# Sums of two parts of a matrix, moved from GpSimd adds to a copying and an accumulating transfer, and two masks built earlier

## The chip, the cores and the metric

The kernel runs on one core of one Trainium2 chip. The metric is the device time of one execution in microseconds (us). TensorE (PE) does the matrix products, VectorE (DVE), ScalarE (ACT) and GpSimd (POOL) the elementwise work. SyncE (SP), ACT and POOL also issue transfers (DMA), and all transfers run on the same 16 DMA engines of the core.

## What is computed

Two layers on a sequence of 512 tokens with 1024 features, and a last normalisation, all in fp32. The second layer, gated linear attention (GLA), stands around the change:

```python
h = h + ssd_mixer(rmsnorm(h, ssd_norm), ...)      # layer 1
h = h + gla_mixer(rmsnorm(h, gla_norm), ...)      # layer 2
return rmsnorm(h, final_norm)

def gla_mixer(u, w_in, w_gate, b_gate, onorm, w_out):
    q, k, v, z, gl = split(u @ w_in)               # gl: 2 x 16 columns, the low-rank gate
    lg = log_sigmoid(gl @ w_gate + b_gate) / 16
    o = gla_scan(q, k, v, lg[0]) + rev(gla_scan(rev(q), rev(k), rev(v), rev(lg[1])))
    return (rmsnorm(o, onorm) * silu(z)) @ w_out
```

## The kernel before

Every product of fp32 matrices is made of three matmuls (`mm3`, L150): each operand is held as a high part (a rounded copy, made by ACT) and a low part (the difference, made by DVE); high times high, high times low and low times high are added in PSUM. For weights, `Weights` loads 512 KB at a time through SP into `wraw` (3 buffers), ACT makes `whi` (L89) and DVE makes `wlo` (L90), 3 buffers each. A buffer of `whi` or `wlo` is free again when PE has read it. For the layer's input u the parts are `uh` and `ul`, 128 x 8 x 512 each, kept for the whole layer.

Layer 1 (SSD) uses the pool `sp`; at its end `proj_out_rows` (L826) adds the layer's output to `h` for each of four blocks of 128 tokens, and `norm2` normalises the block, transposes it on PE and splits it into `uh` and `ul` (L157). Then the pool `gp` takes over the same memory for layer 2.

Layer 2 makes v and z of each head by a product of 2 x 2 blocks with 7 instead of 8 block products (`vz_part`, L881). That needs sums of blocks of u, and these need u itself again, `uf` = `uh` + `ul`, in two tiles (`ufgyh` for features 0 to 511 and `ufgyl` for 512 to 1023), each of 128 x 4 x 512. `uf` is written in four pieces of 128 x 4 x 256 (512 KB), by GpSimd. The order of pieces is: first half of the tokens of `ufgyh`, then of `ufgyl`; second half of `ufgyh`, then of `ufgyl`. From them `sums_of_u` (L848) makes

```python
x = a22 - a21          # L853: second token half of ufgyl minus second token half of ufgyh
y = -x - a11           # L850: a11 is the first token half of ufgyh
# split of y into s2h, s2l and of x into q5h, q5l
x = a11 - a21          # L857, split into s3h, s3l
y = -y - a12           # L850, split into s4h, s4l; a12: first token half of ufgyl
```

In the text "tx" and "ty" are the DVE instructions that write x and y. The program order of the first head is: block products a11 (result `m1`, copied out of PSUM by ACT at L907) and a12 (L893 adds `m1`: `gc`, then split into `vh`, `vl`); `gate_low` (L950), the product for gl with a weight of 768 columns (`pch` with 96 rows, L72 loads its weight); q and k (two more `pch`); the gates (`ptg`, L961, needs `gl` from ACT and DVE, L952 and L953, and `wgs`, the split gate weights of L938 and L939, loaded into `wgr` by SP at L934 after GpSimd has cleared it at L932); then the blocks s2, q5, s3, a22, s4. Products that stay in PSUM take tiles of the tag `mm`, which has 4 buffers (L142): the product of `gate_low` takes the buffer that held the first result of a11, and so starts after the copy of `m1`.

The instructions of an engine run in one fixed order, which a list scheduler has worked out from the program with its own cost estimates. `mk3` (which is the tile `one`, changed in place) and `mle` (`lef` in between) are two 128 x 128 masks; `mle` is first used at L1062.

Of the kernel before, what the change touches and what calls it, by code (L numbers as in the profile page):

```python
# [10 lines left out]
F32 = mybir.dt.float32  # L11
F32R = mybir.dt.float32r
U8 = mybir.dt.uint8
AF = mybir.ActivationFunctionType
ALU = mybir.AluOpType

P = 128
# [30 lines left out]
class Weights:  # L48
# [64 lines left out]
    def next(self):  # L113
        n = len(self.specs) if self.limit is None else self.limit
        while self.n_spl < n and self.n_spl <= self.pos + LOOK_SPL:
            while self.n_raw <= self.n_spl:
                self._load(self.n_raw)
                self.n_raw += 1
            with self.tc.high_priority(offset=SPLIT_AHEAD):
                self._split(self.n_spl)  # L120
            self.n_spl += 1
        self.load_ahead()
        i = self.pos
        for f in self.beside.pop(i, ()):
            f()
        self.pos += 1
        return self.spl.pop(i)


def build(tc, I, out):  # L130
    nc = tc.nc
    ctx = ExitStack()
    with ctx:
        cp = ctx.enter_context(tc.tile_pool(name="cp", bufs=1))
# [36 lines left out]
        def small_loads():  # L171
# [10 lines left out]
        idn = cp.tile([P, P], F32, name="idn")  # L182
        make_identity(nc, idn)
        one = cp.tile([P, P], F32, name="one")
# [3 lines left out]
        ge = cp.tile([P, P], F32, name="ge")  # L188
        nc.gpsimd.affine_select(
            out=ge, in_=one, pattern=[[1, P]], compare_op=ALU.is_ge, fill=0.0, base=0, channel_multiplier=-1  # L190
        )
        mlt = cp.tile([P, P], U8, name="mlt")
        nc.vector.tensor_scalar(out=mlt, in0=ge, scalar1=0.5, scalar2=None, op0=ALU.is_lt)
        rmf = cp.tile([P, L], F32, name="rmf")
        nc.vector.memset(rmf, 1.0)
        nc.vector.memset(rmf.rearrange("p (c l) -> p c l", l=P)[:, :, 0:1], 0.0)
# [55 lines left out]
        class Blocks:  # L252
# [8 lines left out]
            def step(self, n):  # L261
                w = self.w
                dst, src, add = (
                    (w["w1"], self.b11, False),
                    (w["w3"], self.b12, False),
                    (w["w1"], self.b12, True),
                    (w["w3"], self.b22, True),
                    (w["w2"], w["w1"], False),
                    (w["w2"], self.b22, True),
                    (w["w4"], w["w2"], False),  # L270
                    (w["w4"], self.b21, True),
                )[n]
                if add:
                    dma = nc.gpsimd.dma_start(dst, src, accum_op=ALU.add)
                else:
                    dma = nc.gpsimd.dma_start(dst, src)
                tc.add_manual_dep(
                    dma.ins, W.mark.ins.name,
                    mybir.DependencyInfo(mybir.DependencyClass.Sync, mybir.DependencyReason.DATA),
                    reason="pace",  # L280
                )
# [32 lines left out]
        uh = cp.tile([P, KD, L], F32R, name="uh")  # L314
        ul = cp.tile([P, KD, L], F32R, name="ul")
# [48 lines left out]
        def proj_tok(step=lambda: None):  # L364
            pts = [mmb(f"ptk{t}") for t in range(NT)]
            for kk in range(4):
                if kk:
                    step()
                wh, wl = W.next()
                for t in range(NT):  # L370
                    sl = slice(t * P, (t + 1) * P)
                    for j in range(2):
                        k = 2 * kk + j
                        mm3(pts[t], (uh[:, k, sl], ul[:, k, sl]), (wh[j], wl[j]), k == 0, k == KD - 1)
            return pts
# [64 lines left out]
        with tc.tile_pool(name="sp", bufs=1, reuse_waits="tile") as sp:  # L440
# [108 lines left out]
            def proj_group(g, step):  # L549
                b = conv_silu(proj_ch(), 16 + g, "bch")  # L550
                step()
                c = conv_silu(proj_ch(), 24 + g, "cch")
                step()
                x0 = conv_silu(proj_ch(), 2 * g, "xch")
                step()
                x1 = conv_silu(proj_ch(), 2 * g + 1, "xch")
                return b, c, x0, x1

            def z_gate(pts, pool, n):
                zs = []  # L560
                for t in range(NT):
                    if t % 2 == 0:
                        zs.append(pool.tile([P, 2, 512], F32, tag="zs", name=f"zs{t}", bufs=n))
                    z = zs[-1][:, t % 2]
                    nc.scalar.activation(z, pts[t], AF.Tanh, scale=0.5)
                    nc.vector.scalar_tensor_tensor(
                        out=z, in0=z, scalar=1.0, in1=pts[t], op0=ALU.add, op1=ALU.mult
                    )
                return zs
# [224 lines left out]
            for g in range(G + 1):  # L794
                it = iter(scan_group(g - 1, grp.pop(g - 1), zs[(g - 1) // 2])) if g else iter(())
                left = [SCAN_STEPS, 4 * ((g % 2 == 0 and g < G) + (g < G) + (g in (3, 5, 8)))]

                def step():
                    n = -(-left[0] // max(left[1], 1))
                    left[0] -= n  # L800
                    left[1] -= 1
                    for _ in range(n):
                        next(it, None)

                if g < G:
                    if g % 2 == 0:
                        zs[g // 2] = z_gate(proj_tok(step), sp, 3)
                        step()
                    if g == 0:
                        dt_part()  # L810
                        for i in range(3):
                            load_bc(i)
                    grp[g] = proj_group(g, step)
                    step()
                if g in (3, 5, 8):
                    proj_out(yts1(g // 2 - 1 if g < 8 else 2), step)
                for _ in it:
                    pass
# [11 lines left out]
        with tc.tile_pool(name="gp", bufs=1, reuse_waits="tile") as gp:  # L830
            uf = [gp.tile([P, 4, L], F32, tag=tg, name=f"uf{tg}") for tg in ("gyh", "gyl")]
            for th in range(2):
                for hf in range(2):
                    sl = (slice(None), slice(hf * 4, hf * 4 + 4), slice(th * 256, th * 256 + 256))
                    nc.gpsimd.tensor_tensor(
                        out=uf[hf][:, :, sl[2]], in0=uh[sl].bitcast(F32), in1=ul[sl].bitcast(F32), op=ALU.add
                    )


            f1, f2 = slice(0, 256), slice(256, 512)  # L840
# [95 lines left out]
            for d in range(2):  # L936
# [1 line left out]
                nc.scalar.copy(w, wgr[d])  # L938
                nc.vector.tensor_tensor(out=w[32:64], in0=wgr[d][32:64], in1=w[32:64].bitcast(F32), op=ALU.subtract)  # L939
                wgs.append(w)  # L940
            mk3 = one
            nc.vector.tensor_tensor(out=mk3, in0=one, in1=idn, op=ALU.add)
            lef = gp.tile([P, P], F32, tag="xx0", name="lef")
            nc.vector.tensor_tensor(out=lef, in0=mk3, in1=ge, op=ALU.subtract)
            mle = gp.tile([P, P], U8, name="mle")
            nc.vector.tensor_scalar(out=mle, in0=lef, scalar1=0.5, scalar2=None, op0=ALU.is_gt)

            gl = gp.tile([96, L], F32R, name="gl")

# [246 lines left out]
```

## Time and profile before

| | us |
|---|---|
| median of 3 runs | 869.54 (869.53 to 871.34) |
| the profiled execution | 871.69 |
| its span in the trace | 870.0 |
| PE busy in it | 840.9 |
| DVE busy | 676.3 |
| ACT busy | 505.1 |
| POOL busy | 88.5 |

The profiled execution is 2.15 us above the median. The times of the rows below count from the start of its span. A busy time of an engine is a sum over the whole program; what a change in one stretch does is read from who waits for whom in that stretch.

### The profile page before, as it was taken

What the parts mean: (1) busy time and instruction counts of PE and PEld (TensorE: products, weight loads), DVE (VectorE), ACT (ScalarE), POOL (GpSimd) and SP (SyncE); (2) the same over time, 40 slices, a digit from 0 to 9 for tenths busy, and PEclk for the clock granted to TensorE, in tenths of its full rate; (3) what the DMA queues carried; (4) which work ended last, traced back from release to release, by engine and by line L of the source; (5) the groups of instructions that cost most, each with busy time, mean ns of one, the idle gap of its engine ahead of it and who ended that gap; (6) DMA issues with size and microseconds to landing.
All of it is one profiled execution on the core that took longest, in us unless ns stands there. A gap on an engine that the chain in (4) does not pass through costs nothing.

```text
span 870.0 us, 11270 instructions
## 1 busy us (share of the span) xinstructions
PE 840.9 (97%) x3982; PEld 688.3 (79%) x3982; DVE 676.3 (78%) x1046; ACT 505.1 (58%) x1074; POOL 88.5 (10%) x156
## 2 busy tenths in 40 slices
PE   8998999999999999999998999999999999999996
PEld 5786888887888888888877767878888888887875
DVE  6488988999768986589896789859953996399744
ACT  4337587756766566567574547557524762385333
POOL 2002011101101011110101320010001000100012
PEclk9999999999999999999999999999999999999998
DMA  6447848967878687696530236406530662155202
GB/s 211 129 112 298 209 140 234 252 151 231 208 222 218 171 235 199 174 262 170 146 121 25 67 105 178 138 24 185 156 95 27 179 182 74 48 162 177 98 1 97
DMA packets 90198, 132.92 MB, mean 153 GB/s; under 512 B 7969, under 2 KB 49149, under 8 KB 87966
## 3 DMA queue, kind: packets, MB, share of 16 engines
q1 hardware_dynamic: 76844, 83.83, 31.9%
q0 software_dynamic: 11424, 34.74, 17.5%
q10 hardware_dynamic: 1874, 13.64, 4.1%
q8 instruction: 31, 0.51, 0.2%
q14 instruction: 25, 0.20, 0.1%
HBM read 129.96 MB, written 35.78 MB: 191 GB/s over the span
## 4 chain that ended last, share of the span: by engine, by line
PE 63%; DVE 14%; ACT 10%; issue 5%; DMA 3%; POOL 3%; SPq 0%; POOLq 0%; ACTq 0%; DVEq 0%
PE pch L152 5%; PE pch L151 5%; PE pch L153 5%; PE po L153 4%; PE po L151 4%; PE po L152 4%; DVE wlo L90 4%; PE pb L151 3%; PE pb L153 3%; PE pb L152 3%; PE pyi L713 3%; ACT whi L89 3%; PE ptk L151 3%; PE ptk L153 2%; PE ptk L152 2%
## 5 line engine op out<-in xcount | busy, mean ns | idle before, releaser
L90 DVE TENSOR_TENSOR wlo<-wraw,whi 128x1024 fp32r<-128x1024 f32 (+1 forms) x114 | 140.3, 1232 | 56.3 <-ACT whi L89 56.0
L89 ACT CAST whi<-wraw 128x1024 fp32r<-128x1024 f32 (+1 forms) x114 | 118.7, 1041 | 95.7 <-PE pch L152 30.2
L153 PE MATMUL pch<-uh,wlo 128*128 128x512 f32 (+2 forms) x336 | 133.4, 397 | 0.8 <-DVE wlo L90 0.7
L151 PE MATMUL pch<-uh,whi 128*128 128x512 f32 (+2 forms) x336 | 133.7, 398 | 0.0
L152 PE MATMUL pch<-ul,whi 128*128 128x512 f32 (+2 forms) x336 | 132.8, 395 | 0.0
L153 PEld LDWEIGHTS pch<-uh,wlo 128*128 128x128 f32 (+2 forms) x336 | 62.5, 186 | 15.3 <-DVE wlo L90 1.7
L152 PEld LDWEIGHTS pch<-ul,whi 128*128 128x128 f32 (+2 forms) x336 | 62.5, 186 | 13.9 <-issue 0.3
L151 PEld LDWEIGHTS pch<-uh,whi 128*128 128x128 f32 (+2 forms) x336 | 62.5, 186 | 13.5
L541 DVE SCALAR_TENSOR_TENSOR cv<-pch,colA,cv 128x511 f32<-128x511 f32 (+1 forms) x96 | 70.5, 742 | 0.2
L94 ACT ACTIVATE whi<-wraw,colB 128x512 fp32r<-128x512 f32 x58 | 39.1, 717 | 43.8 <-PE pch L152 25.3
L151 PE MATMUL ptk<-whi,uh 128*128 128x512 f32 x128 | 51.4, 406 | 0.0
L153 PE MATMUL ptk<-whi,ul 128*128 128x512 f32 x128 | 50.5, 396 | 0.0
L152 PE MATMUL ptk<-wlo,uh 128*128 128x512 f32 x128 | 50.5, 396 | 0.0
L95 DVE SCALAR_TENSOR_TENSOR wlo<-wraw,colB,whi 128x512 fp32r<-128x512 f32 x58 | 41.7, 748 | 9.9 <-ACT whi L94 8.5
L318 POOL TENSOR_SCALAR rs<-ss 128x2 f32<-128x2 f32 (+1 forms) x32 | 8.6, 268 | 382.0 <-ACT gy L1097 270.2
L680 ACT ACTIVATE bct<-bct,eb 128x128 f32<-128x128 f32 x128 | 42.1, 395 | 6.3 <-DVE bct L677 6.3
L672 ACT ACTIVATE bct<-bct,eb 128x128 f32<-128x128 f32 x128 | 41.2, 395 | 3.4 <-DMA bct<-cumd 3.4
L151 PE MATMUL pb<-whi,uh 128*128 128x512 f32 x96 | 38.7, 403 | 3.2 <-DVE u L893 2.0
L152 PE MATMUL pb<-wlo,uh 128*128 128x512 f32 x96 | 38.3, 399 | 0.0
L153 PE MATMUL pb<-whi,ul 128*128 128x512 f32 x96 | 38.1, 397 | 0.0
L151 PE MATMUL po<-whi,yh 128*128 128x512 f32 x96 | 37.9, 396 | 0.1
L152 PE MATMUL po<-wlo,gyh 128*128 128x512 f32 x96 | 37.9, 395 | 0.0
(308 smaller groups left out, 2022.9 us busy)
## 6 DMA issues: line engine op xcount, KB each, us to landing
wraw<-in_ssd_w_in_dram SPq DMA_DIRECT2D x48, 512.0 KB, 5.7
wsumw<-in_gla_w_in_dram POOLq DMA_DIRECT2D x24, 1024.0 KB, 9.6
wraw<-in_gla_w_in_dram SPq DMA_DIRECT2D x32, 512.0 KB, 3.8
wraw<-wsumw SPq DMA_DIRECT2D x32, 512.0 KB, 3.5
bct<-cumd ACTq DMA_DIRECT2D x13, 1024.0 KB, 6.6
wraw<-in_ssd_w_out_dram SPq DMA_DIRECT2D x16, 512.0 KB, 5.3
wraw<-in_gla_w_out_dram SPq DMA_DIRECT2D x16, 512.0 KB, 4.0
bct<-cumd SPq DMA_DIRECT2D x3, 1024.0 KB, 14.0
```

The source lines that it names most:

```text
L89: self.mark = nc.scalar.copy(vh, raw)
L90: nc.vector.tensor_tensor(out=vl, in0=raw, in1=vh.bitcast(F32), op=ALU.subtract)
L94: self.mark = nc.scalar.mul(hs[j], raw[:, j], g)
L95: nc.vector.scalar_tensor_tensor(out=ls[j], in0=raw[:, j], scalar=g, in1=hs[j].bitcast(F32), op0=ALU.mult, op1=ALU.subtract)
L151: nc.tensor.matmul(pt, lhsT=a[0], rhs=b[0], start=first, stop=False)
L152: nc.tensor.matmul(pt, lhsT=a[0], rhs=b[1], start=False, stop=False)
L153: W.mm = nc.tensor.matmul(pt, lhsT=a[1], rhs=b[0], start=False, stop=last)
L318: nc.gpsimd.tensor_scalar(out=dst, in0=ss, scalar1=mul, scalar2=add, op0=ALU.mult, op1=ALU.add)
L541: nc.vector.scalar_tensor_tensor(out=cv[:, o0:o1], in0=pt[:, o0 + s : o1 + s], scalar=cwt(j, a), in1=cv[:, o0:o1], op0=ALU.mult, op1=ALU.add,)
L672: nc.scalar.activation(bct[:, r], bct[:, r], AF.Identity, bias=TM["eb"][:, cc, i : i + 1])
L680: nc.scalar.activation(et[:, r], et[:, r], AF.Exp, bias=TM["eb"][:, cc, i : i + 1])
L713: nc.tensor.matmul(py[:, q * 256 + r * 64 : q * 256 + (r + 1) * 64], lhsT=et[:, r], rhs=xt[:, cc, r * 64 : (r + 1) * 64], start=True, stop ...
```

## The change

Each of the four adds of GpSimd is replaced by two transfers of 512 KB inside the on-chip memory: one issued by ACT that copies a piece of `uh` into `uf`, and one issued by GpSimd that adds the piece of `ul` to it on its way. The three instructions for the masks move into the loop of layer 1 (at g == 4), with `lef` in a buffer of the tag `jk` and `mle` in the pool that lives for the whole kernel.

```diff
+        mk3, mle = one, cp.tile([P, P], U8, name="mle")
...
+                if g == 4:
+                    nc.vector.tensor_tensor(out=mk3, in0=one, in1=idn, op=ALU.add)
+                    lef = sp.tile([P, P], F32, tag="jk", name="lef", bufs=2)
+                    nc.vector.tensor_tensor(out=lef, in0=mk3, in1=ge, op=ALU.subtract)
+                    nc.vector.tensor_scalar(out=mle, in0=lef, scalar1=0.5, scalar2=None, op0=ALU.is_gt)
...
             for th in range(2):
                 for hf in range(2):
                     sl = (slice(None), slice(hf * 4, hf * 4 + 4), slice(th * 256, th * 256 + 256))
-                    nc.gpsimd.tensor_tensor(
-                        out=uf[hf][:, :, sl[2]], in0=uh[sl].bitcast(F32), in1=ul[sl].bitcast(F32), op=ALU.add
-                    )
+                    nc.scalar.dma_start(uf[hf][:, :, sl[2]], uh[sl].bitcast(F32))
+                    nc.gpsimd.dma_start(uf[hf][:, :, sl[2]], ul[sl].bitcast(F32), accum_op=ALU.add)
...
-            mk3 = one
-            nc.vector.tensor_tensor(out=mk3, in0=one, in1=idn, op=ALU.add)
-            lef = gp.tile([P, P], F32, tag="xx0", name="lef")
-            nc.vector.tensor_tensor(out=lef, in0=mk3, in1=ge, op=ALU.subtract)
-            mle = gp.tile([P, P], U8, name="mle")
-            nc.vector.tensor_scalar(out=mle, in0=lef, scalar1=0.5, scalar2=None, op0=ALU.is_gt)
```

The order of PE's instructions stays as it was. On ACT, DVE, POOL and SP it changes around the passage from layer 1 to layer 2.

ACT before, from the split of the last normalised block on (`whi` of 768 is the weight of `gate_low`; the two `whi` of 1024 after it are those of q and k):

```order
L156 CAST uh<-ptn 128x4x128 [waits PE_49] x2
L89 CAST whi_4542<-wraw_4538 128x768 [waits DMAHW4_49,DMAHW3_49,DMAHW5_49,PE_49,Activation_49]
L907 COPY m_4532<-pb_4486 128x512
L89 CAST whi_4560<-wraw_4558 128x1024 [waits DMAHW6_49,PE_49,Activation_49]
L907 COPY m_4533<-pb_4487 128x512
L156 CAST q5h<-tx 128x1024 [waits DVE_49]
L156 CAST s2h<-ty 128x1024 [waits DVE_49]
L89 CAST whi_4600<-wraw_4598 128x1024 [waits DMAHW7_49,PE_49,Activation_49]
```

ACT in the changed kernel at the same place (DMAHW with a number is the completion counter of one of eight groups of transfers that SP and ACT issue):

```order
L156 CAST uh<-ptn 128x4x128 [waits PE_49] x2
L841 DMA ufgyh<-uh 128x4x256 [waits DVE_49]
L89 CAST whi_4546<-wraw_4542 128x768 [waits DMAHW4_49,DMAHW3_49,DMAHW5_49,PE_49,Activation_49]
L841 DMA ufgyl<-uh 128x4x256
L841 DMA ufgyh<-uh 128x4x256 [waits Activation_49]
L89 CAST whi_4564<-wraw_4562 128x1024 [waits DMAHW6_49,PE_49]
L841 DMA ufgyl<-uh 128x4x256 [waits DMAHW2_49,Activation_49]
L943 CAST wgs_4473<-wgr_4463 96x512 [waits DMAHW3_49,DMAHW4_49,DMAHW1_49,Pool_49]
L943 CAST wgs_4476<-wgr_4468 96x512 [waits DMAHW6_49,DMAHW7_49,DMAHW0_49,Pool_49]
L89 CAST whi_4604<-wraw_4602 128x1024 [waits DVE_49,PE_49]
L912 COPY m_4536<-pb_4490 128x512
L912 COPY m_4537<-pb_4491 128x512
```

The two copies of `m` have moved behind the fourth transfer, both casts of `wgs` and the cast of k's weight.

DVE before, from the low part of the last normalised block on:

```order
L157 TENSOR_TENSOR ul<-ptn,uh 128x4x128 x2
L944 TENSOR_TENSOR lef<-one,ge 128x128
L946 TENSOR_SCALAR mle<-lef 128x128
L90 TENSOR_TENSOR wlo_4543<-wraw_4538,whi_4542 128x768
L853 TENSOR_TENSOR tx<-ufgyl,ufgyh 128x1024
L850 SCALAR_TENSOR_TENSOR ty<-tx,ufgyh 128x1024
L90 TENSOR_TENSOR wlo_4561<-wraw_4558,whi_4560 128x1024
```

DVE in the changed kernel, from the second `gc` on, up to `gl` and the low part of s4 (between `ul` and this piece stand `wlo` of 768, two `wlo` of 1024, two `wgs` and the first `gc`):

```order
L898 TENSOR_TENSOR gc<-pb_4541,m_4537 128x512
L157 TENSOR_TENSOR vl<-gc,vh 128x512
L858 TENSOR_TENSOR tx<-ufgyl,ufgyh 128x1024
L157 TENSOR_TENSOR vl<-gc,vh 128x512
L855 SCALAR_TENSOR_TENSOR ty<-tx,ufgyh 128x1024
L157 TENSOR_TENSOR q5l<-tx,q5h 128x1024
L157 TENSOR_TENSOR s2l<-ty,s2h 128x1024
L862 TENSOR_TENSOR tx<-ufgyh 128x1024
L90 TENSOR_TENSOR wlo_4640<-wraw_4637,whi_4639 128x1024
L855 SCALAR_TENSOR_TENSOR ty<-ty,ufgyl 128x1024
L157 TENSOR_TENSOR s3l<-tx,s3h 128x1024
L952 TENSOR_TENSOR gl<-pch,gl 32x512
```

The first tx has moved back behind seven instructions (two `wlo`, two `wgs`, two `gc`, one `vl`), and `gl` stands behind `s3l`; before, `gl` stood right ahead of `s3l`.

POOL in the changed kernel, where the four adds stood before the two MEMSETs:

```order
L937 MEMSET wgr_4463 96x512 [waits PE_49]
L937 MEMSET wgr_4468 96x512 [waits DMAHW5_49,DMAHW4_49,DMAHW6_49,DMAHW3_49,DMAHW2_49]
L842 DMA ufgyh<-ul 128x4x256 [waits DMAHW1_49,DMAHW7_49,DMAHW0_49,DVE_49]
L842 DMA ufgyl<-ul 128x4x256 [waits DMAHW2_49]
L842 DMA ufgyh<-ul 128x4x256 [waits DMAHW5_49,DVE_49]
L842 DMA ufgyl<-ul 128x4x256 [waits DMAHW2_49,DMASW4_49,DVE_49]
```

Each accumulating transfer waits for the copy into the same piece; the second and the fourth copy count on the same counter, DMAHW2. On SP the six loads of `wgr` now stand ahead of the load of the first `wsumw` block, and the fifth of them waits for DMAHW7, the counter of the first copy.

## Rows read from the trace of the kernel before

**Rows 1.** The page's busy times of the engines over the whole span (us, share, instructions).

```profile
PE 840.9 (97%) x3982; PEld 688.3 (79%) x3982; DVE 676.3 (78%) x1046; ACT 505.1 (58%) x1074; POOL 88.5 (10%) x156
```

**Rows 2.** Busy time of each engine in stretches of the span (from:to in us, length, busy us of each engine, granted TensorE clock, busy share of the DMA engines, GB/s).

```profile
535.00:540.00 5.00, 2.96 (x13) 2.18 (x12) 5.00 (x9) 4.35 (x8) 0.00 (x0) 1.00 0.66 207
540.00:545.00 5.00, 5.00 (x16) 3.94 (x15) 4.19 (x7) 1.85 (x3) 0.00 (x0) 0.66 0.76 206
```

**Rows 3.** Timeline of POOL: the first and the last of the four adds, and the MEMSETs behind them (start, duration, what).

```profile
493.86 3.27 POOL L835 TENSOR_TENSOR ufgyh<-uh,ul 128x1024 f32<-128x1024 f32 x1 [1.58 <-PE ptn L347]
...
501.86 3.12 POOL L835 TENSOR_TENSOR ufgyl<-uh,ul 128x1024 f32<-128x1024 f32 x1
504.92 0.99 POOL L932 MEMSET wgr<- 96x512 f32 x2
```

**Rows 4.** Timeline of DVE beside and behind them.

```profile
495.97 1.31 DVE L944 TENSOR_TENSOR lef<-one,ge 128x128 f32<-128x128 f32 x1
497.32 2.31 DVE L946 TENSOR_SCALAR mle<-lef 128x128 uint8<-128x128 f32 x1
499.55 3.18 DVE L90 TENSOR_TENSOR wlo<-wraw,whi 128x768 fp32r<-128x768 f32 x1
505.01 1.23 DVE L853 TENSOR_TENSOR tx<-ufgyl,ufgyh 128x1024 f32<-128x1024 f32 x1 [2.28 <-POOL ufgyl L835]
...
519.49 0.69 DVE L953 TENSOR_TENSOR gl<-pch,gl 32x512 fp32r<-32x512 f32 x1
```

**Rows 5.** Instructions of the same kinds and sizes elsewhere in the program, by line (ns min/median/max, first and last start).

```profile
L942 DVE TENSOR_TENSOR one<-one,idn x1: 283/283/283, 114.7 to 114.7; 128x128 f32<-128x128 f32 x1
L193 DVE TENSOR_SCALAR mlt<-ge x1: 222/222/222, 5.0 to 5.0; 128x128 uint8<-128x128 f32 x1
L640 DVE TENSOR_TENSOR xw<-xt,ww x16: 949/952/957, 89.8 to 440.6; 128x768 f32<-128x768 f32 x16
```

**Rows 6.** Timeline of DVE at the place in layer 1 to which the masks move.

```profile
234.21 1.23 DVE L90 TENSOR_TENSOR wlo<-wraw,whi 128x1024 fp32r<-128x1024 f32 x1 [0.51 <-ACT whi L89]
```

**Rows 7.** Timeline of PE: the end of block a12 and the start of `gate_low`, q's third matmul, the gates, the end of block s3, and block a22.

```profile
501.18 0.39 PE L153 MATMUL pb<-whi,ul 128*128 128x512 f32 x1
501.41 0.39 PE L151 MATMUL pch<-uh,whi 128*96 128x512 f32 x1
...
502.78 0.48 PE L153 MATMUL pch<-uh,wlo 128*96 128x512 f32 x1 [0.75 <-DVE wlo L90]
...
508.69 0.51 PE L153 MATMUL pch<-uh,wlo 128*128 128x512 f32 x1
...
519.00 0.39 PE L153 MATMUL pch<-uh,wlo 128*128 128x512 f32 x1
520.24 0.72 PE L961 MATMUL ptg<-gl,wgs 96*128 96x512 f32 x2 [0.84 <-DVE gl L953]
...
537.04 0.39 PE L153 MATMUL pb<-whi,s3l 128*128 128x512 f32 x1
539.47 0.47 PE L151 MATMUL pb<-whi,uh 128*128 128x512 f32 x1 [2.04 <-DVE u L893]
...
541.41 0.63 PE L152 MATMUL pb<-wlo,uh 128*128 128x512 f32 x1
541.84 0.63 PE L153 MATMUL pb<-whi,ul 128*128 128x512 f32 x1
```

**Rows 8.** Timeline of ACT around the first block products.

```profile
493.87 1.26 ACT L156 CAST uh<-ptn 128x512 fp32r<-128x512 f32 x2 [1.03 <-PE ptn L347]
496.21 0.84 ACT L89 CAST whi<-wraw 128x768 fp32r<-128x768 f32 x1 [1.07 <-PE pb L153]
496.95 0.58 ACT L907 COPY m<-pb 128x512 f32<-128x512 f32 x1
498.93 1.05 ACT L89 CAST whi<-wraw 128x1024 fp32r<-128x1024 f32 x1 [1.40 <-issue]
```

**Rows 9.** Transfers of the whole program by line (count, KB each, median us from issue to landing).

```profile
wraw<-in_ssd_w_in_dram SPq DMA_DIRECT2D x48, 512.0 KB, 5.7
wraw<-wsumw SPq DMA_DIRECT2D x32, 512.0 KB, 3.5
wgr<-in_gla_w_gate_dram SPq DMA_DIRECT2D x6, 32.0 KB, 1.8
```

**Rows 10.** DMA from 421 to 434 us, when one accumulating transfer (of 1024 KB, issued by POOL at 421.3) and one load of weights were in flight: queues (packets, MB, share of 16 engines over the 13 us) and issues (KB, us to landing).

```profile
q0 software_dynamic: 528, 1.05, 50.3%
q1 hardware_dynamic: 272, 0.52, 12.5%
...
wsumw<-in_gla_w_in_dram POOLq DMA_DIRECT2D x1, 1024.0 KB, 10.5
wraw<-in_ssd_w_out_dram SPq DMA_DIRECT2D x1, 512.0 KB, 9.1
```

**Rows 11.** The plain (not accumulating) transfers of 1024 KB that POOL issues, us from issue to landing.

```profile
DMA to landing us min/median/max: 5.4/6.0/9.9
```

**Rows 12.** Stretches as in rows 2, behind a wait of PE of 0.98 us at 788.04.

```profile
788.00:792.00 4.00, 3.02 (x14) 2.52 (x14) 4.00 (x7) 1.53 (x2) 0.00 (x0) 1.00 0.40 148
```

**Rows 13.** Stretches as in rows 2, later in layer 2.

```profile
550.00:560.00 10.00, 10.00 (x49) 8.40 (x49) 9.28 (x14) 6.33 (x10) 0.00 (x0) 1.00 0.57 159
...
820.00:830.00 10.00, 10.00 (x46) 8.18 (x45) 5.44 (x8) 3.36 (x6) 0.18 (x1) 1.00 0.05 20
```

## The prediction

> **What bounds the kernel now.** I read the page's busy times first: PE is busy for 97% of the span [rows 1], so a change shows in the time only where it makes PE wait, or takes a wait away, or moves the clock. Then the timelines of PE, DVE, POOL and ACT around the passage from layer 1 to layer 2. There DVE sets the pace from 496 to 539 us. The reader is to see three things.
>
> First, while the four adds run on GpSimd, from 493.86 to 504.98 [rows 3], DVE is slow: `lef` takes 1.31 us, `mle` 2.31 and the low part of a weight of 768 columns 3.18 [rows 4], against 0.28, 0.22 and 0.95 for the same kinds and sizes elsewhere [rows 5]. PE waits for that last one: its third matmul of `gate_low` starts at 502.78 where the step of 0.23 would put it at 501.87 [rows 7], 0.91 lost.
>
> Second, tx starts at 505.01, after 2.28 us of waiting for the last add, and from there DVE works without a real pause. PE waits for its results twice more: at the gates, 519.23 to 520.24 (1.0 lost, `gl` ends at 520.18 [rows 4, 7]), and at block a22, where 2.04 us are idle until 539.47.
>
> Third, behind that last wait the granted clock falls: 0.66 over 540 to 545 [rows 2], matmuls 0.43 us apart instead of 0.23 [rows 7], which is the lower of the two levels, 1.2 GHz. In the timeline eight matmuls run so, 8 x 0.20 = 1.6 us. Behind a wait of 0.98 us the clock stays at 1.00 [rows 12]. So a wait of two microseconds costs 1.6 more, one of one microsecond nothing more.
>
> From 550 on PE is busy for practically all of each 10 us [rows 13]: what is lost or won before stays to the end.
>
> **What the change removes.** The adds, so DVE's slowness and its wait for them. The low part of the 768 columns then starts when its high part is done, 496.21 + 0.84 = 497.05 [rows 8], and ends at 498.0 instead of 502.73: PE's 0.91 goes, and so does 0.26 at 508.69 (the next low part, late for the same reason [rows 7]). The masks in layer 1 cost 0.28 + 0.22 = 0.50 us of DVE, in front of an instruction that waits 0.51 us for ACT [rows 6]: hidden; without that cover 0.5 us.
>
> **What it adds on ACT and PE.** `gate_low` starts after the first copy of `m`, which ended at 497.5, long before it was needed. In the new order that copy stands behind the fourth transfer (waits for the second copy to land), two casts of `wgs` (wait for loads of which the fifth waits for the first copy to land) and the cast of k's weight. That cast needs a buffer that PE frees at the end of block a12, 501.6 [rows 7]. With no other delay: 501.6 + 1.05 + 0.5 [rows 8] = 503.2, this is the lower bound. With the transfers: the first copy is issued at 495.1, behind the casts of `uh` [rows 8]. A transfer of 512 KB lands 3.5 to 5.7 us after issue [rows 9]; here it has a load of weights and the next copies beside it, so I take 4.9: 500.0. Then the last two loads of `wgr` (0.8 to issue, 1.8 to land [rows 9]): 502.6. The second copy, issued at 497.05, lands at 501.9 by the same price. Casts of `wgs` 1.1, of k's weight 1.0, copy of `m` 0.5: **505.4**. PE starts `gate_low` 4.0 us later than at 501.41. It gives back 0.91 and 0.26, and k's product ends at 519.23 + 2.8 = 522.0; with the clock's fall behind a wait of four microseconds (1.6) at 523.6.
>
> **What it adds ahead of tx.** tx needs the third and fourth pieces, so the last accumulating transfer. Price of one: no row shows an accumulate inside SBUF. The nearest is the one of 1024 KB in DRAM [rows 10]: 528 packets took 50.3% of 13 us on 16 engines, 6.5 us, and it landed 10.5 us after issue, thus 4 us around the data, of which about 2 was the load beside it. If the time goes with the bytes, 512 KB are 3.3 us of all 16 engines. If it goes with packets (512 again, of 1 KB), 6.5. If SBUF accumulates as a plain transfer, half of 5.4 [rows 11] with all around it, 2.7. The plain load in the same window took 12.5% of 13 us = 1.6 us for 512 KB [rows 10], and an accumulate reads twice: twice 1.6 is 3.2. I take 3.3, the value in the middle that two rows give.
>
> Now they queue. Copies 4 x 1.6 = 6.4, accumulates 4 x 3.3 = 13.2, the load of k's weight 1.6: 21.2 us of work on the same 16 engines, from about 496 us, and each accumulate starts only when its copy has landed and GpSimd has issued it. That a neighbour slows a transfer is in the rows: a load beside the accumulate landed after 9.1 us instead of 3.5 to 5.7 [rows 9, 10]. So the last one lands at about 496 + 21 = **517**. tx starts at 517 instead of 505. The Trainium skill (DMA: Bandwidth & Descriptors, section "Issuing engines are not separate DMA queues") says that transfers issued by different engines run on the same 16 DMA engines and interleave; the 9.1 us agree, and it speaks against this change.
>
> **What that costs.** DVE had work of 5.4 us between tx and `gl` that now stands ahead of tx (two `wlo`, two `wgs`, two `gc`, one `vl`). From tx to the end of `gl` there remain tx, `vl`, ty, q5l, s2l, tx, `wlo`, ty, s3l and `gl`: 8 x 1.14 + 0.6 + 0.7 = 10.4 us. `gl` is ready at 527.4 and PE does the gates at 527.5 instead of 520.24: 7.3 late (PE itself was there at 523.6, so its own delay hides behind this). From the gates to the end of s3 PE needs 17.0 us [rows 7], and 1.6 more with the clock low behind the wait: 546.1. DVE's side takes 539.47 - 520.18 = 19.3 us from `gl` on, less s3l, now done before it: 18.2, thus 545.6. So PE starts block a22 at 546.1, 6.6 late and without the wait; the old fall of the clock (1.6) goes. **Sum: 6.6 - 1.6 = 5.0 us slower.** Against the profiled execution, 871.69, that is 876.7; that one was 2.15 above the median, and I set the sum on the median: 869.54 + 5.0 = **874.5**. In short, with T the start of tx, the change is T - 512.
>
> **The rivals.**
> *Faster: the transfers are quick.* If a copy lands 2.8 us after issue and an accumulate 4, the fourth copy is issued at 500.0 (behind the cast of q's weight), lands at 502.9, and T is 507. Then `gate_low` starts at 503.3, 1.9 later, minus 0.91 and 0.26: the gates at 520.0, PE at a22 at 537.0 with DVE done by 536, thus 2.4 early, and 1.6 of clock: 4.0 faster, 2.4 if the wait at `gate_low` already lowers the clock. About 3.2: 866.3. It decides at T below 510 together with `gate_low` before 504. For it: the DMA share was low here. Against it: rows 10. The Trainium skill (the same page, section "Anatomy of one DMA — SWDGE (gpsimd) path") has 2.0 us plus the bytes at 436 GB/s; an estimate from that page is 3.2 us for 512 KB, which leads to this rival. By it the 1024 KB of rows 10 would take 4.4 us; the trace has 10.5.
>
> *No change: T between 510.3 and 513.7.* Accumulates of 2 us of engine time give 4 x 1.3 = 5 less than mine: T = 512, 869.5.
>
> *Much slower: the price goes with packets.* 4 x 3.2 = 13 us more: T = 530, 887.5. Against it: the plain load's time goes with bytes, twice of it is the accumulate's.
>
> **Chances.** Forecast (T 514 to 524, 871.5 to 881.5) 0.62; much slower 0.08; no change 0.15; faster 0.15. The rival of no change spills to either side: faster by over 0.2% 0.17, within 0.2% (1.7 us, about what a measurement of this kernel can tell from no change) 0.12, slower 0.71. The range goes from 867, the middle of the fast rival's reach, to 884: half of the fast rival and nearly all of the much slower one are left out, 0.15.
>
> **What would show it.** Right: `lef` and `mle` near 0.3 and 0.2 us in layer 1; `wlo` of 768 near 0.95 and no PE wait behind it; a PE wait for ACT's copy of `m` before `gate_low` of 2 to 5 us; tx idle before an accumulating transfer and starting at 514 or later; PE waiting for `gl` for some 4 us; a clock below 1.00 behind these waits and at 1.00 around 541 + 6. Wrong: tx before 511, or a landing of the accumulates under 4.5 us (then the price of one was too high), or `gate_low` within 2 us of 501.4 (then the new order on ACT costs less), or a later stretch in which PE gets back what it lost.

## The result and the profile after

The changed kernel takes **882.42 us** against 870.09 before (four runs of each), a ratio of 1.0141 with a 95% interval of 1.0121 to 1.0162: 12.3 us slower. Every time of a kernel is the median of its fast runs; single executions of 970 to 3684 us are left out. I had predicted 874.5, 5.0 slower. The direction and the mechanism came out; the size was more than twice what I forecast.

The busy times of the page hardly tell: PE is busy 1.1 us longer, DVE 5.5 and POOL 5.9 shorter.

```profile
span 880.7 us, 11278 instructions
PE 842.0 (96%) x3982; PEld 689.8 (78%) x3982; DVE 670.8 (76%) x1046; ACT 506.1 (57%) x1074; POOL 82.6 (9%) x156
```

PE's waits between 490 and 560 us tell it (operation, what it waited for, us in total, times, longest).

```profile
PE pch L151 <- ACT m L912: 6.8, 1, 6.8
PE ptg L960 <- DVE gl L952: 6.5, 1, 6.5
...
PE pb L151 <- DVE u L898: 0.4, 1, 0.4
```

Before, PE lost 0.9 and 0.26 at the low parts of weights, 1.0 at the gates, and 2.04 at block a22 with a fall of the clock behind it [rows 2, 7]. Now it stands 6.8 us ahead of `gate_low`, 6.5 us at the gates and 0.4 at block a22. The granted clock falls behind both waits, to about half, the lower level of 1.2 GHz. Behind block a22, which is at 552 now, it stays at 1.00: the old fall of [rows 2] is gone (windows: busy time of PE, PEld, DVE, ACT and POOL, granted clock, DMA share, GB/s).

```profile
505.00:510.00 5.00, 2.75 (x7) 1.88 (x8) 4.32 (x6) 3.74 (x6) 1.28 (x1) 0.52 1.10 257
...
530.00:535.00 5.00, 2.39 (x6) 1.94 (x7) 4.96 (x6) 4.34 (x6) 0.00 (x0) 0.50 0.35 105
...
550.00:560.00 10.00, 9.58 (x43) 7.64 (x42) 9.49 (x13) 5.29 (x8) 0.00 (x0) 1.00 0.65 187
```

Where both waits come from stands in the timelines of DVE, ACT's queue and POOL (start, duration, what, idle time before).

```profile
495.97 0.96 DVE L90 TENSOR_TENSOR wlo<-wraw,whi 128x768 fp32r<-128x768 f32 x1 [1.02 <-ACT whi L89]
...
521.91 1.22 DVE L858 TENSOR_TENSOR tx<-ufgyl,ufgyh 128x1024 f32<-128x1024 f32 x1 [11.96 <-DMA ufgyl<-ul]
...
531.78 0.69 DVE L952 TENSOR_TENSOR gl<-pch,gl 32x512 fp32r<-32x512 f32 x1
```

```profile
493.45 0.76 ACTq L841 DMA_DIRECT2D ufgyh<-uh  x1
...
495.12 0.62 ACTq L841 DMA_DIRECT2D ufgyl<-uh  x1
...
503.42 0.60 ACTq L841 DMA_DIRECT2D ufgyl<-uh  x1
...
505.16 0.62 ACT L943 CAST wgs<-wgr 96x512 fp32r<-96x512 f32 x1 [0.35 <-DMA wgr<-in_gla_w_gate_dram]
...
506.63 1.06 ACT L912 COPY m<-pb 128x512 f32<-128x512 f32 x2
```

```profile
502.08 1.38 POOL L842 DMA_DIRECT2D ufgyh<-ul  x1 [9.98 <-DMA wraw<-in_gla_w_in_dram]
503.72 1.27 POOL L842 DMA_DIRECT2D ufgyl<-ul  x1 [0.26 <-issue]
505.40 1.28 POOL L842 DMA_DIRECT2D ufgyh<-ul  x1 [0.41 <-issue]
515.06 1.27 POOL L842 DMA_DIRECT2D ufgyl<-ul  x1 [8.38 <-DMA ufgyl<-uh]
```

ACT issues the fourth copy only at 503.42, when the second has landed. Its last wait ahead of the copies of `m` is for a load of `wgr`, until 505.16: the last two of these loads go out on SP only when the first copy has landed. The copies of `m` stand behind both and end PE's first wait. On GpSimd the first accumulating transfer goes out at 502.08, when the first copy and a load of weights have landed. The fourth copy needs until 515 to land, the last accumulating transfer goes out behind it, and tx starts when that one has landed.

In this execution the passage comes 1.1 us earlier than in the profile of before (the last two `ul` start at 493.67 against 494.77); "on the same clock" below means with these 1.1 us added. To compare kernels I use **x**, the time from the start of the low part of 768 columns to the start of tx. My forecast of tx at 517, with that low part at 497.05, is x = 20.0; measured here are 25.9.

What the transfers share the 16 engines with shows in the DMA queues from 495 to 522 us (packets, MB, share of 16 engines over 27 us; the last line shows the loads of `wsumw` issued in this time, KB each and us to landing): q0 are the accumulating transfers, q10 the copies, q1 the loads of SP.

```profile
q0 software_dynamic: 2112, 2.10, 48.6%
q1 hardware_dynamic: 2031, 2.29, 29.7%
q10 hardware_dynamic: 2112, 2.10, 26.9%
...
wraw<-wsumw SPq DMA_DIRECT2D x3, 512.0 KB, 6.7
```

In us of all 16 engines that is 13.1 for the accumulates (3.28 each), 7.3 for the copies (1.8 each), and 8.0 for the loads: 28.4 (packets overlap a little, so that the shares add to over 100%), where my sum had 13.2 + 6.4 + 1.6 = 21.2. The loads are the surprise: beside the one weight that I counted, three loads of `wsumw`, the weights of the next block products, ran here.

### The profile page after: what moved, and what is told of

Same layout as the page of the kernel before. It is cut to its first block, busy times and chain, and to the rows that moved or that the text cites. A ratio compares the mean times of both kernels' runs of the same rounds, so it can differ in the third digit from the quotient of the medians.

```text
span 880.7 us, 11278 instructions
## 1 busy us (share of the span) xinstructions
PE 842.0 (96%) x3982; PEld 689.8 (78%) x3982; DVE 670.8 (76%) x1046; ACT 506.1 (57%) x1074; POOL 82.6 (9%) x156
## 4 chain that ended last, share of the span: by engine, by line
PE 68%; DVE 12%; ACT 9%; issue 4%; DMA 4%; POOL 2%; POOLq 0%; ACTq 0%; DVEq 0%
PE pch L152 5%; PE pch L151 5%; PE pch L153 5%; PE po L151 4%; PE po L152 4%; PE po L153 4%; PE pb L151 4%; PE pb L152 4%; PE pb L153 4%; DVE wlo L90 3%; PE ptk L151 3%; PE ptk L153 3%; PE ptk L152 3%; PE pyi L714 3%; ACT whi L89 2%
## 5 line engine op out<-in xcount | busy, mean ns | idle before, releaser
L90 DVE TENSOR_TENSOR wlo<-wraw,whi 128x1024 fp32r<-128x1024 f32 (+1 forms) x114 | 137.9, 1211 | 58.5 <-ACT whi L89 58.2
L95 DVE SCALAR_TENSOR_TENSOR wlo<-wraw,colB,whi 128x512 fp32r<-128x512 f32 x58 | 41.6, 746 | 10.1 <-ACT whi L94 8.7
L153 PE MATMUL po<-whi,yl 128*128 128x512 f32 x96 | 37.9, 396 | 0.0
L712 ACT ACTIVATE xc<-xt,coef 128x64 f32<-128x64 f32 x128 | 33.8, 338 | 6.9 <-DVE coef L630 6.8
```

The lines of the kernel that those rows point to most:

```text
L90: nc.vector.tensor_tensor(out=vl, in0=raw, in1=vh.bitcast(F32), op=ALU.subtract)
L95: nc.vector.scalar_tensor_tensor(out=ls[j], in0=raw[:, j], scalar=g, in1=hs[j].bitcast(F32), op0=ALU.mult, op1=ALU.subtract)
L153: W.mm = nc.tensor.matmul(pt, lhsT=a[1], rhs=b[0], start=False, stop=last)
L712: nc.scalar.mul(xc[:, q, k], xt[:, cc, k], coef[:, cc, r : r + 1])
```

## The experiments

Each text that begins a run was written before that run; its theory A and rival B say what the time would be by either. The ratio goes by runs of the kernel before in the same round, whose medians were 869.2 to 870.1. "Plain copies" add nothing: these kernels leave u's high part out of the sums. "Late loads" hold four loads of `wsumw` back until the first tx has run.

| kernel | x, us | PE ahead of `gate_low` | PE at the gates | time, us | ratio to before |
|---|---|---|---|---|---|
| masks alone | 8.0 | none | 0.8 | 869.52 | 1.0001 (0.998 to 1.0022) |
| changed kernel | 25.9 | 6.8 | 6.5 | 882.42 | 1.0141 (1.0121 to 1.0162) |
| transfers alone | 25.6 | 7.1 | 6.5 | 882.79 | 1.0152 (1.0124 to 1.0181) |
| all issued by GpSimd | 24.8 | 2.5 | 11.3 | 882.87 | 1.0149 (1.0111 to 1.0187) |
| plain copies only | 23.2 | 6.6 | 3.5 | 879.78 | 1.0105 (1.0080 to 1.0131) |
| late loads | 22.3 | 7.1 | 2.9 | 878.54 | 1.0119 (1.0068 to 1.0170) |
| late loads, again | 22.4 | 7.0 | 3.2 | 878.23 | 1.0095 (1.0072 to 1.0118) |
| second half first | 19.7 | 6.7 | 2.7 | 878.44 | 1.0096 (1.0071 to 1.0120) |
| late, second half first | 15.9 | 6.9 | 0.2 | 875.10 | 1.0063 (1.0043 to 1.0083) |
| late, plain copies | 16.0 | 6.7 | none | 874.57 | 1.0058 (1.0037 to 1.0080) |
| late, plain, all by GpSimd | 16.3 | none | none | 869.36 | 0.9997 (0.9976 to 1.0017) |

### Each part of the change alone

In the first kernel the masks alone move: the adds stay on GpSimd as before.

> The four adds on GpSimd stay as before; only the masks (`lef`, `mle`) are built in layer 1. Theory A (the loss of 12.3 us is all in the transfers): 868.5 to 870.5 us against 870.1 before; tx still starts when the last add ends, so `gl` and the gates stay where they were, and the 0.91 us of PE behind the low part of 768 columns goes only into the wait for the gates. Rival B (the masks in layer 1 stand in front of something that layer 1 waits for): 871.5 or more. Rival C (less for DVE to do beside the adds brings tx and `gl` forward too): below 868.5.

The time is 869.52, no difference, which is theory A. The masks' new place costs and brings nothing.

In the second the transfers stay, and the three instructions for the masks are back in layer 2.

> The sums of u by copying and accumulating transfers as in the changed kernel, the masks built in layer 2 as before. Theory A (the loss is all in the transfers): 881.5 to 884 us, as the changed kernel; the masks take 0.5 us of DVE where it waits 12 us for tx anyway, and tx starts as late as there (about 522). Rival B (a part of the loss comes from the masks' new place): 881 or less.

The time is 882.79, as the changed kernel, which is theory A. The whole loss is in the transfers.

### Which of the two waits sets the time

In this kernel GpSimd issues all eight transfers (the cut diff leaves out the list `pieces`, which holds the same four pieces in the same order):

```diff
-            for th in range(2):
-                for hf in range(2):
-                    nc.scalar.dma_start(uf.., uh..)
-                    nc.gpsimd.dma_start(uf.., ul.., accum_op=ALU.add)
...
+            for hf, sl in pieces:
+                nc.gpsimd.dma_start(uf.., uh..)
+            for hf, sl in pieces:
+                nc.gpsimd.dma_start(uf.., ul.., accum_op=ALU.add)
```

> As the changed kernel, but GpSimd issues the four copies too, all ahead of the four accumulating transfers, so that ACT no longer stands behind a copy that has to land; PE's wait of 6.8 us ahead of `gate_low` (for the first copy of `m`) falls to 1 to 3 us. Theory A (the start of tx sets the time; what PE loses at `gate_low` it would lose at the gates anyway): tx starts at 519 to 524, PE's wait for `gl` grows from 6.5 to about 11 us, and the time stays at 880 to 884 us. Rival B (the wait at `gate_low` has its own price): 876 to 878.5 us, the 4 to 5 us of that wait given back.

```profile
PE ptg L964 <- DVE gl L956: 11.3, 1, 11.3
PE pch L151 <- ACT m L916: 2.5, 1, 2.5
```

This is theory A: 4.3 us less ahead of `gate_low`, 4.8 more at the gates, the same time. tx itself comes 1.1 us earlier by x, but GpSimd now clears `wgr` behind the transfers, so that two `wgs` stand between tx and `gl` on DVE, and `gl` ends 11.6 us after the start of tx instead of 10.6. As long as tx is this late, the order on ACT costs nothing of its own.

### What delays tx: the loads of weights

The edit makes the next four loads of weights, those of `wsumw`, wait for the first tx (cut):

```diff
+        W.late = range(len(W.specs), len(W.specs) + 4)
...
+            if i in self.late:
+                self.tc.add_manual_dep(dma.ins, self.tx.ins.name, ...)
```

> As the changed kernel with every engine's order the same; four loads of weights (`wsumw`, 512 KB each, of which three to four ran between 500 and 520 beside the transfers) now wait until the first tx has run. Theory A (what my sum left out is their time on the 16 DMA engines: the load queue took 8.0 us of each engine between 495 and 522 where I counted 1.6): tx starts at 515 to 518 instead of 522, and the time is 876 to 879 us, if the late loads come in time for their casts (PE needs the first of them only behind the gates). Rival B (the accumulating transfers are slow by themselves or wait for their own queue): tx stays at 521 to 523 and the time at 881 to 884.

The kernel ran a second time:

> The kernel with the four late loads once more, in more runs, since its first time (877.8 to 881.7 us) left open how much of the 3.7 us by which tx came forward reaches the end. Theory A (what tx gains, the time gains): 3 to 5 us below the changed kernel, 877.5 to 879.5 us, a ratio to before of 1.008 to 1.011. Rival B (a later wait takes it back): 881 or more, 1.0125 or more.

The DMA queues of this kernel from 495 to 522 us, and its tx:

```profile
q0 software_dynamic: 2112, 2.10, 54.6%
q10 hardware_dynamic: 2112, 2.10, 27.3%
q1 hardware_dynamic: 1369, 1.17, 14.7%
```

```profile
495.46 0.96 DVE L97 TENSOR_TENSOR wlo<-wraw,whi 128x768 fp32r<-128x768 f32 x1 [1.02 <-ACT whi L96]
...
517.74 1.23 DVE L866 TENSOR_TENSOR tx<-ufgyl,ufgyh 128x1024 f32<-128x1024 f32 x1 [8.01 <-DMA ufgyl<-ul]
```

x falls from 25.9 to 22.3 (22.4 the second time), and PE's wait at the gates from 6.5 to 2.9 (3.2). The first three runs, 877.84 to 881.67, have their median in the range of A, 878.54, but the interval of their ratio also holds B; the second time 878.23 at 1.0095, with 1.0118 as the upper end, is theory A. So 3.6 of the 5.9 us by which x was longer than I had it are the loads of `wsumw`. I put what is left, 22.3 against 20.0, down to the copies' and the accumulates' longer time on the engines: 7.4 and 14.7 us here, 2.5 more than my 6.4 and 13.2. No run tries this apart.

### The price of an accumulating transfer

```diff
-                    nc.gpsimd.dma_start(uf.., ul.., accum_op=ALU.add)
+                    nc.gpsimd.dma_start(uf.., ul..)
```

> As the changed kernel with every engine's order the same; the four accumulating transfers only copy (the sum of the high and low parts is left out of the computation, u being replaced by its low part). Theory A (an accumulating transfer takes twice a plain one's time of the 16 DMA engines: 3.28 against 1.82 us): the second set of transfers takes 7 us instead of 13, tx starts at 514 to 517 and the time is 875 to 878 us. Rival B (latency: what counts is the chain of a copy landing, an issue by GpSimd, and a landing): tx stays at 520 to 523, 880 to 884.

```profile
q0 software_dynamic: 576, 2.10, 21.8%
```

```profile
515.86 0.75 POOL L842 DMA_DIRECT2D ufgyl<-ul  x1 [9.84 <-DMA ufgyl<-uh]
```

Four plain transfers of the same bytes, in 576 packets instead of 2112, take 5.9 us of the engines instead of 13.1. But x falls by only 2.8, to 23.2, and the time to 879.78, between the two forecasts: neither theory alone is right. The last of them is still issued at 515.86, because the fourth copy lands no earlier. With late loads as well this chain is shorter:

> The four loads late, and the accumulating transfers only copying (u's high part is left out of the sums again). Theory A (the engines' work sets tx: the two gains, 3.7 and 2.8 us, add): 19 to 20 us from the low part of 768 columns to tx; 874.5 to 877 us. Rival B (the fourth copy's late issue and landing set it, whichever of the two is taken away): 21.5 us or more, 877.5 to 880 us.

```profile
505.43 0.75 POOL L850 DMA_DIRECT2D ufgyl<-ul  x1 [0.90 <-DVE wgs L952]
```

```profile
503.60 0.62 ACT L951 CAST wgs<-wgr 96x512 fp32r<-96x512 f32 x1 [2.08 <-DMA wgr<-in_gla_w_gate_dram]
```

```profile
494.47 0.96 DVE L97 TENSOR_TENSOR wlo<-wraw,whi 128x768 fp32r<-128x768 f32 x1 [1.01 <-ACT whi L96]
...
510.46 1.23 DVE L866 TENSOR_TENSOR tx<-ufgyl,ufgyh 128x1024 f32<-128x1024 f32 x1 [2.06 <-DMA ufgyl<-ul]
```

The last piece goes out at 505.43 and x is 16.0: a gain of 9.9, more than the sum of 3.6 and 2.8 that theory A had, and outside both forecasts of x. With plain copies alone the last piece waited for the fourth copy, until 515.86; with late loads alone it went out at 508.84, but then stood behind accumulates; each of the two hid a part of what the other brings. The time, 874.57, is where A had it, but for another reason: with x = 16.0 my rule (loss = x - 15) would give 1 us, and it lost 5.0. PE waits for nothing at the gates now; the 6.7 us ahead of `gate_low` are left. ACT issues the fourth copy at 500.19 here, 5.7 us after the low part of 768 columns began (7.5 in the changed kernel), yet it still waits until 503.60 for a load of `wgr`. That load, and not the fourth copy, ends last ahead of the copies of `m`.

### The order of the pieces

```diff
-            for th in range(2):
+            for th in (1, 0):
```

> As the changed kernel, but the pieces go in the other order: the second half of the tokens first, so that tx needs the first two accumulating transfers and not the last two. In the changed kernel's trace the second of them landed at 516.4 and the third at 519.1, the fourth at 521.9. Theory A (tx's start sets the time, and it hangs on the place in the transfers' queue alone): tx starts at 515 to 518, the first ty, which needs the third, at about 519, 4.5 us before it does in the changed kernel; 876.5 to 879 us. Rival B (the sums that need the last pieces set the time as well, so the order of the pieces is worth nothing): 881 to 884.

```profile
515.92 1.23 DVE L858 TENSOR_TENSOR tx<-ufgyl,ufgyh 128x1024 f32<-128x1024 f32 x1 [9.21 <-DMA ufgyl<-ul]
...
519.40 1.22 DVE L855 SCALAR_TENSOR_TENSOR ty<-tx,ufgyh 128x1024 f32<-128x1024 f32 x1
```

This is theory A: tx starts at 515.9, ty at 519.4, and the time is 878.44. Together with late loads:

> The four loads late and the second half of the tokens first. From the start of the low part of 768 columns to tx it took 25.9 us in the changed kernel, 22.3 with the late loads, 19.7 with the second half first. Theory A (both act through the same 16 engines' work ahead of tx, so they add): 15.5 to 17 us, with the later pieces and ty behind it some 3 us earlier than with the second half first alone; 873 to 876.5 us. Rival B (what is left is the chain of a copy's landing, an issue and an accumulate's landing, which the loads do not lengthen there): 18.5 to 20 us, 877 to 880 us.

x = 15.9 and the time is 875.10, A again. And again the loss stops at 5 to 6 us while PE hardly waits at the gates.

### What the last 5 us are

The next kernel has late loads and plain copies, all transfers issued by GpSimd, and the clearing and loading of `wgr` put ahead of them, so that neither a copy nor a load of `wgr` stands ahead of the copies of `m` on ACT:

> As the kernel with late loads and plain copies (u's high part is left out of the sums), which was 5.0 us slower than before although tx started 16.0 us after the low part of 768 columns, by my rule a loss of 1 us. Here GpSimd issues all eight transfers and the loads of `wgr` stand where they did, so that ACT copies `m` early, as in the kernel before. Theory A (what is left of the loss there is PE's wait of 6.7 us for that copy ahead of `gate_low`, hidden only as long as PE has to wait at the gates anyway): that wait falls to 0 to 1 us, tx starts within 2 us of the same place, and the time is 868 to 872 us. Rival B (the rest of the loss comes from elsewhere: the late loads, or the clock): 873.5 us or more.

```profile
PE pb L158 <- ACT whi L96: 0.9, 1, 0.9
PE pb L159 <- DVE wlo L97: 0.8, 1, 0.8
```

```profile
511.14 0.69 DVE L963 TENSOR_TENSOR gl<-pch,gl 32x512 fp32r<-32x512 f32 x1
514.90 1.23 DVE L876 TENSOR_TENSOR tx<-ufgyl,ufgyh 128x1024 f32<-128x1024 f32 x1 [3.07 <-DMA ufgyl<-ul]
```

Neither of the two waits is left, x is 16.3 as without this edit (16.0), and the loss is gone: 869.36, ratio 0.9997. This is theory A's time, but the edit does more than A says: `gl` now stands ahead of tx on DVE, so that the gates no longer depend on tx at all. How much of the 5 us ACT's copy of `m` is worth by itself was not tried apart. In the kernel with late loads and plain copies `gl` ended at 521.02 and PE reached the gates at 525.03, so by my estimate some 4 of the 5 us are PE's late start of `gate_low`. So two paths lead to the gates, one through tx and one through ACT's copy of `m`. By the waits of PE the first sets the time where x is about 20 or more, and the second, at a loss of 5 to 6 us, where x is 16.

### A version that beats both

Here there are no transfers. The adds are back on GpSimd, the masks stay in layer 1, and the adds of the second half of the tokens come first:

> No transfers: the four adds on GpSimd as before, the masks in layer 1, and the adds of the second half of the tokens ahead of those of the first half, so that tx needs the first two adds instead of all four. Theory A (DVE's wait for the adds, 7 us with the masks gone, is what delays `gl` and PE behind it): tx starts about 4.5 us earlier (at 498 to 500), the first ty one add later, PE's waits for `gl` (0.8) and at block a22 (2.0, and 1.6 of clock) shrink, 865 to 868 us against 869.8 before. Rival B (DVE's instructions on SBUF are held until the add that runs beside them has ended, as `lef`, `mle` and the low part of 768 columns were before, so DVE gains nothing while adds run): 869 to 871.

The time is 870.80, ratio 1.0000 (0.9984 to 1.0017), which is theory B. DVE and POOL in turn, in two views of this kernel:

```profile
503.81 3.41 DVE L864 TENSOR_TENSOR tx<-ufgyl,ufgyh 128x1024 f32<-128x1024 f32 x1 [2.29 <-POOL ufgyl L840]
507.33 3.24 DVE L861 SCALAR_TENSOR_TENSOR ty<-tx,ufgyh 128x1024 f32<-128x1024 f32 x1
```

```profile
500.66 3.11 POOL L840 TENSOR_TENSOR ufgyl<-uh,ul 128x1024 f32<-128x1024 f32 x1
503.74 2.40 POOL L840 TENSOR_TENSOR ufgyh<-uh,ul 128x1024 f32<-128x1024 f32 x1
506.10 3.39 POOL L840 TENSOR_TENSOR ufgyl<-uh,ul 128x1024 f32<-128x1024 f32 x1
```

tx is 1.2 us of work (its duration in the changed kernel) and takes 3.41: it ends at 507.22, 1.1 behind the end of the third add at 506.14. ty ends 1.1 behind the end of the fourth. Each of these instructions stood until the add beside it was over.

So the adds themselves move to DVE, and nothing else changes from the last kernel:

```diff
-                return nc.gpsimd.tensor_tensor(
+                return nc.vector.tensor_tensor(
```

> No transfers and no adds on GpSimd: DVE does the four adds itself (the second half of the tokens first), 1.14 us each by its other instructions of this size, 4.6 together; the masks in layer 1. With the masks gone DVE waits 7.0 us for GpSimd's adds. Theory A (DVE's path from the end of layer 1 to `gl` sets the time): `gl` ends 2 to 3 us earlier, PE's waits at 502 (1.1), for `gl` (0.8) and at block a22 (2.0 and the clock behind it) shrink or go; 865 to 868.5 us against 869.8. Rival B (4.6 us more work on the engine that sets the pace there): 870 to 873.

**865.45 us, ratio 0.9947 (0.9926 to 0.9968)**: theory A, at its lower end. Without GpSimd or a transfer, u is whole when DVE has done four instructions of 1.2 us; this is the end of the last one, and what follows it.

```profile
498.92 1.22 DVE L840 TENSOR_TENSOR ufgyl<-uh,ul 128x1024 f32<-128x1024 f32 x1
...
504.05 1.21 DVE L864 TENSOR_TENSOR tx<-ufgyl,ufgyh 128x1024 f32<-128x1024 f32 x1
...
509.90 0.69 DVE L958 TENSOR_TENSOR gl<-pch,gl 32x512 fp32r<-32x512 f32 x1
```

```profile
PE pb L151 <- DVE u L904: 1.5, 1, 1.5
```

`gl` ends 15.9 us after the low part of 768 columns began (494.65); with the adds on GpSimd and the masks moved it was 23.1, so the gain at `gl` is 7 us where I had 2 to 3. A part of it is a new order: `gl` stands ahead of the second tx and of s2l now. PE can use less: counted from the start of the last two `ul`, it starts block a22 after 41.6 us instead of 44.7, 3.1 earlier. The time fell by 4.6 us, with an interval of 2.8 to 6.4; where the other 1.5 come from, if they are real, these rows don't show. The waits at `gate_low` and at the gates are gone.

## Why the prediction was wrong in size

**Removed work: right.** The low part of 768 columns took 0.96 us and no PE wait stands behind it; the masks were free in layer 1.

**`gate_low`: 4.0 us late forecast, 6.9 measured** (507.25, or 508.35 on the same clock, against 501.41). Two landings came later than I had them. A copy was to land 4.9 us after issue, by my choice; the first three took 7.9 to 8.2 and the fourth 11.0. The loads of `wgr` were to land after 1.8 us, and none took less than 3.6. The list of what stands ahead of the copy of `m` was right (its terms add to 505.2, not to 505.4), with the load of `wgr` behind the first copy as its last wait, as I had it.

**The price of an accumulate: right.** It is 3.28 us of the 16 engines for 512 KB, forecast 3.3, and 3.7 with late loads. It goes with the bytes, not with the packets: 528 packets took 6.5 us with 1024 KB [rows 10] and 3.28 with 512 KB.

**T: 517 forecast, 523.0 on the same clock. This step failed most.** I added the work of the 16 engines, but let only one load of SP take part: that term was 1.6 us and measured 8.0. SP's loads of `wsumw`, three of 512 KB, stood in the same stretch. In the trace SP's loads of weights wait for DVE's `wlo`, thus for a free buffer, and nothing in the change puts them behind the transfers. With these loads made late, tx came 3.6 us earlier by x; I put the rest down to the longer time per copy and per accumulate, which is not shown apart. The Trainium skill (DMA: Bandwidth & Descriptors, section "Issuing engines are not separate DMA queues") says that transfers of different issuers run on the same 16 engines and interleave; the trace agrees (28.4 us of work in 27). I applied it to two issuers of three and to one load of the third.

**From tx on: right, but for the clock.** `gl` ended 10.56 us after the start of tx (10.4 forecast), and block a22 came 19.0 us after the gates (18.6). On the same clock block a22 starts at 552.7, 13.3 us late where I had 6.6; 6.0 of the difference are T. The fall of the clock at 541 is gone, the 1.6 us that I took off. With the 1.1 us that this execution was ahead already, that makes 10.6, and the two spans lie 10.7 apart.

But I set the sum on the median, and there the 1.6 us are not safe. I read from one place that a wait of two microseconds costs 1.6 more. With the masks alone PE has the same wait at block a22 (timeline of PE and windows of that kernel), and the clock stays at 1.00:

```profile
537.03 0.47 PE L151 MATMUL pb<-whi,uh 128*128 128x512 f32 x1 [2.04 <-DVE u L899]
```

```profile
535.00:540.00 5.00, 2.97 (x13) 2.53 (x14) 5.00 (x8) 2.89 (x5) 0.00 (x0) 1.00 0.76 210
540.00:545.00 5.00, 5.00 (x23) 4.14 (x23) 4.51 (x7) 2.64 (x3) 0.00 (x0) 1.00 0.57 147
```

With the second half of the adds first it stays there too, behind 2.0 us. So the wait does not always bring the fall. Between the medians the loss, 12.3, lies between the 11.7 with this term and the 13.3 without it; how many executions of the kernel before have the fall is not shown.

**"In short, the change is T - 512": only half a rule.** It holds where tx is the later path. Below, `gate_low` sets a floor, which I had at PE's readiness for the gates, 523.6, and so below the forecast; it is at a loss of 5 to 6 us, as the kernels at x = 16 show. Had only T been right, at x = 20, the loss would have been some 7 to 8 us, an estimate between the kernels at 16 and at 22.3 in the table, not 5. Both failures have one root: how late transfers land beside others.

**The rivals.** The faster rival asked for copies that land 2.8 us after issue and accumulates in 4; they took 8 to 11 and 7 to 14. The estimate of 3.2 us from the fit in the Trainium skill (DMA: Bandwidth & Descriptors, section "Anatomy of one DMA — SWDGE (gpsimd) path") does not hold here, where transfers share the engines. "Much slower", by packets, was 5.1 us too high (887.5) and wrong in its mechanism.

## What to carry to other kernels

Before an operation is moved to a transfer, list every transfer that will be in flight in the same stretch, with the prefetches of all other queues, and add up their time on the shared engines; the sum, and not the latency of one transfer alone, is about the least that the last one needs. A transfer that must wait for another adds to it: with plain copies alone the engines had 20.2 us of work from 495 us on, and tx started 24.2 us after 495. Then follow each queue on which a transfer that has to wait is issued: what stands behind it on that engine is a second path, which shows only when the first is cured. Where an engine waits for a helper longer than the helper's work would take on it, try the work there: four adds on DVE, 4.9 us, removed a wait of 7.

## What the runs showed of the hardware

**An add of GpSimd holds back a DVE instruction on SBUF whole, until the add is over.** In the kernel before, `lef`, 0.28 us of work, began beside the first add and ended 0.15 us after it [rows 3, 4]; with the masks moved, the low part of 768 columns began at 494.61, as an add ended (494.66), and took its normal 0.96, while the add that began at 494.62 took 3.20. So the slowness that I read as a rate ("DVE is slow") is a wait for the end of the add in progress. An add can wait for DVE in turn: by their ends, those of 3.1 to 3.4 us instead of 2.4 began while an instruction of DVE still ran. The Trainium skill (SBUF — State Buffer, section "SBUF: two separate sides") has it so for a DVE instruction with two inputs in SBUF beside a GpSimd instruction that reads SBUF: a port pair that the two share, an exclusive lock, held for the whole instruction; the trace agrees, with 3.41 and 3.24 us for tx and ty above.

**A transfer that is issued has not begun.** In the changed kernel three accumulates were issued from 502.08 to 506.7, but in the two microseconds from 504.5 only loads moved data (DMA queues, 504.5 to 506.5 us; q0 would be the accumulates):

```profile
q1 hardware_dynamic: 317, 0.62, 102.4%
```

The first packets of the accumulates come in the next two microseconds, when the loads thin out:

```profile
q0 software_dynamic: 206, 0.21, 65.6%
q1 hardware_dynamic: 129, 0.23, 39.4%
```

With late loads the first accumulate is issued at 501.44, and its first packets come between 504 and 505. What decides the turn between queues, no run here shows.
